# Hybrid decoder step: the last token group's FFN takes every other weight tile unsplit from its input and splits it on chip

## The chip, the cores and the metric

The kernel runs on one NeuronCore of one Trainium2 chip. The metric is the device time of one execution in microseconds (us); of several runs the median is taken. Besides the timed runs there is one profiled execution, and all durations, waits and clocks below come from its trace. In the trace PE is the matmul engine (PEld its weight loads), ACT the scalar engine, DVE the vector engine, and SP the engine from whose queue nearly all DMAs are issued. Tiles are named as in the program, with buffer numbers left out.

## The reference, cut to what matters

One layer of a decoder is applied to a prompt of 2048 tokens and to 8 single sample tokens. The first half of the layer mixes tokens (windowed attention beside a state-space scan); the second half is a SwiGLU FFN, and the change lies there:

```python
x = x + jnp.concatenate([a, s_out], axis=-1) @ w_out
h2 = rms_norm(x, norm2_w)
x = x + (jax.nn.silu(h2 @ w_gate) * (h2 @ w_up)) @ w_down   # 1024 -> 2816 -> 1024
...
yp = rms_norm(yp, final_norm_w)
```

All of it is float32.

## The kernel before

**Groups.** The tokens are cut into six groups that go one after the other through all stages: 256 tokens, four times 384, and last 264 (256 prompt tokens and the 8 samples). Each group needs all the weights again, since they don't fit on chip.

**Three matmuls for one.** The PE works in a faster, shortened float format. So each operand is split into a high part and a low rest, and a product is three matmuls: high by high, high by low, low by high (`mm3`). For an activation both parts come from ACT and DVE. For a weight tile there are two ways, both in `weight` (line 198):

- *raw*: a tile of 128x512 floats (256 KB; 128x384, 192 KB, for most of `wd`) is loaded from the input tensor into a buffer `wraw` (line 206, four buffers). ACT copies it, rounded, into the high half of a buffer `w` (line 207; the program's tag is `w2`, five buffers), and DVE subtracts that from the raw tile into the low half (line 209).
- *kept*: a tile that was split once has been stored to DRAM with both halves (line 213). From then on one DMA of 512 KB (384 KB for most of `wd`) fetches both halves into a `w` buffer (line 203), and ACT and DVE have nothing to do.

A third of the tiles is stored at its first use, a third at its second, a third at its third. So the first group takes all its tiles raw, the second and third take fewer and fewer, and from the fourth group on every tile is kept.

**The FFN stage** (`stage_f`, line 975). It goes through 22 blocks of 128 hidden features. For each, two tiles of the gate (`wg`) and then two of the up projection (`wu`) are multiplied into PSUM; ACT takes a tanh of the gate (line 1014), DVE multiplies (lines 1000, 1003), ACT and DVE split the result into the two halves of `hc` (lines 1004, 1008). The blocks form seven chunks, six of three and one of four. After the first block of a chunk, the down projection of the chunk before follows: eight `wd` tiles, each for one 128-row slice of the output, added to `x` by DVE (line 993). In the last group a `wg` or `wu` tile feeds 12 matmuls of 264 columns, a `wd` tile 9 (12 in the last chunk): 88 and 56 tiles, 144 in all, 1584 matmuls.

**Beside it.** While the last group's FFN begins, the final norm of the fifth group (`stage_z`) runs: two matmuls, a chain on ACT and DVE (lines 692 to 700), eight scalings on DVE (line 1041), and four stores of 384 KB from the SP queue (line 1043).

**Order.** A scheduler puts each engine's instructions into a fixed order when the program is built; each engine then works through its queue in that order. A load into a buffer waits until the buffer's last reader is done, and everything behind it in the SP queue waits too. With five `w` buffers, the load of a tile can be issued when the PE has finished the tile five places ahead of it.

Of the kernel before, what the change touches and what calls it, by code (L numbers as in the profile page):

```python
# [10 lines left out]
F32 = mybir.dt.float32  # L11
# [3 lines left out]
ALU = mybir.AluOpType  # L15
# [57 lines left out]
def hymba(ctx: ExitStack, tc: tile.TileContext, I: dict, O: dict, groups):  # L73
# [4 lines left out]
    NMAX = max(nb * P + (NS if s else 0) for nb, s in groups)  # L78
# [9 lines left out]
    def T(shape, dtype=F32, tag=None, bufs=1):  # L88
        cnt[0] += 1
        nm = f"{tag}_{cnt[0]}"  # L90
        return sb.tile(shape, dtype, tag=tag, name=nm, bufs=bufs)
# [5 lines left out]
    def DR(shape, tag, bufs=1):  # L97
        cnt[0] += 1
        return dr.tile(shape, F32, tag=tag, name=f"{tag}_{cnt[0]}", bufs=bufs)

    V, S, G, PE, SP = nc.vector, nc.scalar, nc.gpsimd, nc.tensor, nc.sync
# [83 lines left out]
    def later(n, fn):  # L185
        due.append((clock[0] + n, len(due) + cnt[0] * 1e-6, fn))
# [7 lines left out]

    wn, kept, seen = [0], {}, {}

    def weight(name, at, w=512):
        t = T([P, 1024], F32R, tag="w2", bufs=5)[:, :2 * w]  # L200
        hi, lo = t[:, :w], t[:, w:]
        if (name, at) in kept:
            SP.dma_start(t.bitcast(F32), kept[name, at])
            return hi, lo
        raw = T([P, 512], tag="wraw", bufs=4)[:, :w]
        SP.dma_start(raw, I[name][at] if name != "wd" else I[name][:, at:at + w])
        S.activation(hi, raw, AF.Copy)  # L207
        e = V
        e.tensor_tensor(lo, raw, hi.bitcast(F32), ALU.subtract)  # L209
        k = seen[name, at] = seen.get((name, at), len(seen) % 3) - 1  # L210
        if k < 0:
            d = kept[name, at] = DR([P, 2 * w], f"{name}{len(kept)}")
            later(2, lambda: SP.dma_start(d, t.bitcast(F32)))
        return hi, lo

    def std(name, u):

        r = []
        for h in range(2):
            hi, lo = weight(name, (u, h))  # L220
            r += [(hi[:, k * P:(k + 1) * P], lo[:, k * P:(k + 1) * P]) for k in range(4)]
        return r
# [751 lines left out]

    def stage_f(g):
        N, x1, h2 = g["N"], g["x1"], g["h2"]
        if not hid:
            hid.append(T([P, 2 * (FC + 1) * NMAX], F32R, tag="hc").rearrange("p (a o t) -> p a o t", a=2 * (FC + 1), o=1))
        hid3 = hid[0]

        def down(c, end=False):
            fs, n = chunks[c], len(chunks[c]) * P

            for ms in ([[0, 1, 2], [3], [4], [5], [6], [7]] if end else [[m] for m in range(KT)]):
                w = [weight("wd", c_off[c] + m * n, n) for m in ms]
                ps = [PS("d") for m in ms]
                jobs = [(i, m) for i in range(len(fs)) for m in range(len(ms))]
                for i, m in sorted(jobs, key=lambda e: (e[0] == len(fs) - 1, e[1], e[0])):
                    wi = tuple(t[:, i * P:(i + 1) * P] for t in w[m])
                    s = fs[i] % (FC + 1)  # L990
                    mm3(ps[m][:, :N], wi, (hid3[:, s], hid3[:, FC + 1 + s]), 0, N, i == 0, i == len(fs) - 1)
                for m, p in zip(ms, ps):
                    V.tensor_tensor(x1[:, m, :N], p[:, :N], x1[:, m, :N], ALU.add)  # L993
                    if end:
                        norm_sum(g, x1, sq, m, N, 0 if g is gs[-1] else 1)
                if ms[-1] % 4 == 3 or end:
                    yield
# [48 lines left out]
    gs, b0, off, prev = [], 0, 0, None  # L1046
    for nb, smp in groups:
        g = dict(nb=nb, smp=smp, b0=b0, off=off, N=nb * P + (NS if smp else 0), prev=prev)
        g["early"] = prev is None
        gs.append(g)  # L1050
        off += g["N"]
        b0 += nb
        prev = g
    assert b0 == NB
    n = len(gs)
    kinds = {"I": stage_x0, "X": stage_x, "A": stage_a, "K": stage_k, "B": stage_b, "P": stage_p, "Q": stage_q, "Y": stage_y,
             "S": stage_s, "O": stage_o, "H": stage_h, "F": stage_f, "Z": stage_z}
    made = {}

# [163 lines left out]
```

## Time and profile before

| | us |
|---|---|
| median of 3 runs (2373.48 to 2375.46) | 2374.78 |
| the profiled execution's own time | 2376.97 |
| its span in the trace | 2375.2 |
| PE busy, share of the span | 2290.4 (96%) |
| DVE busy | 1382.0 (58%) |
| ACT busy | 911.8 (38%) |
| bytes moved by DMA, mean rate | 628.96 MB, 265 GB/s |
| last group's FFN: first and last matmul start | 2151.2 and 2361.7 |

PE is marked busy for nearly all of the span, but its matmuls overlap in the record: one of 264 columns is shown for about 0.28 us, and the next starts 0.12 us after it when nothing is late. So the busy share hides short delays; the number of matmuls in a stretch against its length shows them. What ends the program after the last matmul of the FFN (norm, scaling, stores) takes about 13 us and is not touched.

### The profile page before, as it was taken

Reading aid. Unit: us, or ns where it says so; the run is one execution under the profiler, and the core shown is the slowest. Engines: PE = TensorE matmul, PEld = TensorE weight load, DVE = VectorE, ACT = ScalarE, POOL = GpSimd, SP = SyncE. Lnnn points to the kernel's source line nnn. Section 1 sums busy time; section 2 is a strip of 40 time slices with the busy share of each in tenths; the row PEclk is TensorE's granted clock in tenths of the full one; section 3 lists DMA queues with packets and bytes.
Section 4 is the critical chain, followed back from the end, with each engine's and each line's share of the span. In section 5 each row is a group of like instructions: output and inputs, shape, how many; then the busy total and the mean of one; then the engine's idle time right before and its main releaser. Section 6 shows DMA issues by size and latency. Waiting matters only on the chain.

```text
span 2375.2 us, 39240 instructions
## 1 busy us (share of the span) xinstructions
PE 2290.4 (96%) x14633; PEld 2230.5 (94%) x14633; DVE 1382.0 (58%) x3173; ACT 911.8 (38%) x1989; POOL 31.5 (1%) x109
## 2 busy tenths in 40 slices
PE   7999998999999999999999999999999999999997
PEld 6889887999999999999999999999989999998997
DVE  8987978665778555366745535554455574233223
ACT  6766666544436343332622332242233213122001
POOL 1000000000000000000000000000000000000000
PEclk9999999999999999999999999999999999999999
DMA  9766677888767778877887887777798798888997
GB/s 318 253 208 237 198 255 242 302 309 283 238 212 246 240 252 290 275 265 252 268 289 269 281 259 233 218 230 234 244 315 295 228 302 274 254 284 314 340 329 259
DMA packets 227226, 628.96 MB, mean 265 GB/s; under 512 B 24323, under 2 KB 57916, under 8 KB 226892
## 3 DMA queue, kind: packets, MB, share of 16 engines
q1 hardware_dynamic: 226892, 626.26, 79.4%
q8 instruction: 116, 1.90, 0.3%
q14 instruction: 74, 0.61, 0.1%
q10 hardware_dynamic: 144, 0.20, 0.0%
HBM read 516.67 MB, written 110.21 MB: 264 GB/s over the span
## 4 chain that ended last, share of the span: by engine, by line
PE 77%; DMA 11%; DVE 6%; ACT 3%; issue 2%; SPq 0%; ACTq 0%; DVEq 0%
PE psd L104 72%; PE psm L104 5%; DVE w L209 2%; DMA w<-wi 2%; DMA w<-wg 1%; DMA w<-wu 1%; DMA w<-wd 1%; DMA wraw<-in_wu_dram 1%; DMA wraw<-in_wg_dram 1%; ACT w L207 1%; DMA wraw<-in_wd_dram 1%; DMA wraw<-in_wi_dram 1%; ACT big L587 0%; DMA wraw<-in_wo_dram 0%; PE psm L607 0%
## 5 line engine op out<-in xcount | busy, mean ns | idle before, releaser
L104 PE MATMUL psd<-bhi,w 128*128 128x384 f32 (+1 forms) x4448 | 1089.0, 326 | 29.4 <-DVE w L209 8.5
L104 PEld LDWEIGHTS psd<-bhi,w 128*128 128x128 f32 x4448 | 781.9, 189 | 42.1 <-DVE w L209 12.4
L104 PE MATMUL psd<-blo,w 128*128 128x384 f32 (+1 forms) x2224 | 719.1, 324 | 0.1
L104 PE MATMUL psd<-hc,w 128*128 128x384 f32 (+2 forms) x3168 | 521.4, 321 | 15.6 <-DMA w<-wd 3.9
L104 PE MATMUL psd<-ahi,w 128*128 128x384 f32 (+1 forms) x2272 | 516.3, 314 | 20.6 <-DMA w<-wi 7.3
L104 PEld LDWEIGHTS psd<-hc,w 128*128 128x128 f32 x3168 | 496.8, 188 | 25.8 <-DVE w L209 5.2
L104 PEld LDWEIGHTS psd<-blo,w 128*128 128x128 f32 x2224 | 421.1, 189 | 1.4 <-DVE blo L338 0.3
L104 PEld LDWEIGHTS psd<-ahi,w 128*128 128x128 f32 x2272 | 386.2, 189 | 30.6 <-DMA w<-wi 7.1
L207 ACT ACTIVATE w<-wraw 128x512 fp32r<-128x512 f32 (+1 forms) x391 | 232.2, 602 | 338.4 <-PE psd L104 203.0
L104 PE MATMUL psd<-alo,w 128*128 128x384 f32 (+1 forms) x1136 | 355.5, 313 | 0.0
L209 DVE TENSOR_TENSOR w<-wraw,w 128x512 fp32r<-128x512 f32 (+1 forms) x391 | 252.9, 653 | 101.8 <-ACT w L207 98.3
L993 DVE TENSOR_TENSOR x<-psd,x 128x384 f32<-128x384 f32 (+2 forms) x336 | 168.5, 510 | 132.8 <-PE psd L104 132.1
L104 PEld LDWEIGHTS psd<-alo,w 128*128 128x128 f32 x1136 | 215.0, 189 | 1.5 <-issue 0.2
L1014 ACT ACTIVATE tmp<-psd 128x384 f32<-128x384 f32 (+2 forms) x132 | 59.8, 453 | 346.0 <-PE psd L104 345.9
L1000 DVE SCALAR_TENSOR_TENSOR tmp<-tmp,psd 128x384 f32<-128x384 f32 (+2 forms) x132 | 66.7, 505 | 176.3 <-ACT tmp L1014 176.2
L1003 DVE SCALAR_TENSOR_TENSOR tmp<-psd,tmp 128x384 f32<-128x384 f32 (+2 forms) x132 | 67.5, 512 | 167.2 <-PE psd L104 166.8
L1004 ACT ACTIVATE hc<-tmp 128x384 fp32r<-128x384 f32 (+2 forms) x132 | 64.4, 488 | 250.4 <-DVE tmp L1003 249.7
L381 DVE SCALAR_TENSOR_TENSOR x<-tmp,cols,x 128x384 f32<-128x384 f32 (+1 forms) x144 | 80.5, 567 | 37.9 <-ACT x L403 23.2
L317 ACT ACTIVATE tmp<-x 128x384 f32<-128x384 f32 (+2 forms) x84 | 40.5, 489 | 139.1 <-DVE x L941 102.1
L1008 DVE TENSOR_TENSOR hc<-tmp,hc 128x384 fp32r<-128x384 f32 (+2 forms) x132 | 67.6, 512 | 29.4 <-ACT hc L1004 29.3
L320 DVE TENSOR_TENSOR sq<-sq,tmp 128x384 f32<-128x384 f32 (+2 forms) x119 | 61.5, 517 | 34.9 <-ACT tmp L317 33.8
L587 ACT ACTIVATE big<-big,sm 128x256 f32<-128x256 f32 (+1 forms) x128 | 62.4, 489 | 20.8 <-DVE sm L581 20.6
(259 smaller groups left out, 1722.7 us busy)
## 6 DMA issues: line engine op xcount, KB each, us to landing
w<-wu SPq DMA_DIRECT2D x177, 512.0 KB, 4.6
w<-wg SPq DMA_DIRECT2D x175, 512.0 KB, 4.8
w<-wi SPq DMA_DIRECT2D x144, 512.0 KB, 4.9
w<-wd SPq DMA_DIRECT2D x192, 384.0 KB, 4.1
w<-wo SPq DMA_DIRECT2D x65, 512.0 KB, 4.5
wraw<-in_wg_dram SPq DMA_DIRECT2D x89, 256.0 KB, 3.6
wu<-w SPq DMA_DIRECT2D x44, 512.0 KB, 4.1
wg<-w SPq DMA_DIRECT2D x44, 512.0 KB, 3.4
```

Source lines behind the costliest of these rows:

```text
L104: PE.matmul(o, l, r, start=start, stop=stop)
L207: S.activation(hi, raw, AF.Copy)
L209: e.tensor_tensor(lo, raw, hi.bitcast(F32), ALU.subtract)
L320: e.tensor_tensor(sq[:, :N], sq[:, :N], t[:, :N], ALU.add)
L381: V.scalar_tensor_tensor(acc, raw[:, j:j + NP], cwc(j, t), acc, ALU.mult, ALU.add)
L587: S.activation(sc[kv][:, r, :W], sc[kv][:, r, :W], AF.Exp, bias=ng[:, h:h + 1], accum_out=den[:, h:h + 1])
L993: V.tensor_tensor(x1[:, m, :N], p[:, :N], x1[:, m, :N], ALU.add)
L1000: V.scalar_tensor_tensor(t[:, :N], t[:, :N], 1.0, pg[:, :N], ALU.add, ALU.mult)
L1003: V.scalar_tensor_tensor(t[:, :N], pu[:, :N], 0.5, t[:, :N], ALU.mult, ALU.mult)
L1004: S.activation(hh[:, 0, :N], t[:, :N], AF.Copy)
L1008: e.tensor_tensor(hl[:, 0, :N], t[:, :N], hh[:, 0, :N].bitcast(F32), ALU.subtract)
L1014: S.activation(t[:, :N], pg[:, :N], AF.Tanh, scale=0.5)
```

## The change

A flag `again` is set when the last group's FFN begins (its token count is below the maximum and its index above 2; no other group meets both). While it is set, every second call of `weight` takes the raw way although the kept copy exists: a DMA of 256 or 192 KB in place of 512 or 384 KB, then the copy on ACT and the subtraction on DVE. Nothing is stored again. Since each projection asks for an even number of tiles, these are the first of the two tiles of each `wg` and `wu` step, and the even ones of the eight `wd` tiles: 72 of 144. The values are the same. The rest of the diff only names things; all line numbers behind the function move by 3 or 4.

```diff
+    kept, seen, again, turn = {}, {}, [False], [0]
     def weight(name, at, w=512):
         t = T([P, 1024], F32R, tag="w2", bufs=5)[:, :2 * w]
         hi, lo = t[:, :w], t[:, w:]
-        if (name, at) in kept:
+        turn[0] += 1
+        if (name, at) in kept and not (again[0] and turn[0] % 2):
             SP.dma_start(t.bitcast(F32), kept[name, at])
             return hi, lo
...
         S.activation(hi, raw, AF.Copy)
-        e = V
-        e.tensor_tensor(lo, raw, hi.bitcast(F32), ALU.subtract)
+        V.tensor_tensor(lo, raw, hi.bitcast(F32), ALU.subtract)
+        if (name, at) in kept:
+            return hi, lo
...
     def stage_f(g):
         N, x1, h2 = g["N"], g["x1"], g["h2"]
+        again[0] = g["N"] < NMAX and g["i"] > 2
...
-        g["early"] = prev is None
+        g["early"], g["i"] = prev is None, len(gs)
```

**Place 1, the SP queue at the beginning of the last group's FFN**, where the fifth group's results are stored (`out_yT_dram`). Before:

```order
1334 L203 DMA w_3633_22668<-wu_2003_11659 128x1024
1335 L1043 DMA out_yT_dram<-x_3083_18836 128x2x384
1336 L203 DMA w_3634_22670<-wu_525_2923 128x1024
1337 L1043 DMA out_yT_dram<-x_3083_18836 128x2x384
1338 L203 DMA w_3636_22700<-wg_1308_7443 128x1024
1339 L1043 DMA out_yT_dram<-x_3083_18836 128x2x384
1340 L203 DMA w_3637_22702<-wg_2010_11703 128x1024
1341 L1043 DMA out_yT_dram<-x_3083_18836 128x2x384
```

The same place now (`wraw` is a raw tile, `w` a kept one):

```order
1337 L208 DMA wraw_22792<-in_wd_dram 128x384
1338 L205 DMA w_3640_22688<-wu_525_2923 128x1024
1339 L1047 DMA out_yT_dram<-x_3083_18836 128x2x384 x3
1340 L205 DMA w_3644_22723<-wg_2010_11703 128x1024
1341 L1047 DMA out_yT_dram<-x_3083_18836 128x2x384
1342 L208 DMA wraw_22821<-in_wd_dram 128x384
1343 L208 DMA wraw_22853<-in_wd_dram 128x384
1344 L205 DMA w_3649_22761<-wu_1319_7501 128x1024
```

Three stores now stand in a row ahead of the kept tile 3644 (the second `wg` tile of the fourth block), and the raw tiles stand about eight tiles ahead of their use: the raw `wd` tile 22792 is queued ahead of the kept `wu` tile 3640.

**Place 2, DVE around a down projection of the last group's FFN** (L1003 and L1008 are the last steps of a hidden block, L993 the addition of one of the eight `wd` results). Before:

```order
2698 L1003 SCALAR_TENSOR_TENSOR tmp_23498<-psd_23505,tmp_23498 128x264
2699 L1008 TENSOR_TENSOR hc_2636<-tmp_23498,hc_2636 128x264
2700 L1000 SCALAR_TENSOR_TENSOR tmp_23561<-tmp_23561,psd_23536 128x264
2701 L1003 SCALAR_TENSOR_TENSOR tmp_23561<-psd_23569,tmp_23561 128x264
2702 L1008 TENSOR_TENSOR hc_2636<-tmp_23561,hc_2636 128x264
2703 L1000 SCALAR_TENSOR_TENSOR tmp_23625<-tmp_23625,psd_23600 128x264
2704 L1003 SCALAR_TENSOR_TENSOR tmp_23625<-psd_23633,tmp_23625 128x264
2705 L1008 TENSOR_TENSOR hc_2636<-tmp_23625,hc_2636 128x264
2706 L993 TENSOR_TENSOR x_3504_21708<-psd_23662,x_3504_21708 128x264
2707 L993 TENSOR_TENSOR x_3504_21708<-psd_23675,x_3504_21708 128x264
2708 L993 TENSOR_TENSOR x_3504_21708<-psd_23688,x_3504_21708 128x264
```

Now, from the last hidden block's steps on:

```order
2743 L1004 SCALAR_TENSOR_TENSOR tmp_23736<-tmp_23736,psd_23711 128x264
2744 L210 TENSOR_TENSOR w_3797_23803<-wraw_23804,w_3797_23803 128x384
2745 L1007 SCALAR_TENSOR_TENSOR tmp_23736<-psd_23747,tmp_23736 128x264
2746 L210 TENSOR_TENSOR w_3802_23833<-wraw_23834,w_3802_23833 128x384
2747 L1012 TENSOR_TENSOR hc_2636<-tmp_23736,hc_2636 128x264
2748 L997 TENSOR_TENSOR x_3504_21708<-psd_23779,x_3504_21708 128x264
2749 L997 TENSOR_TENSOR x_3504_21708<-psd_23792,x_3504_21708 128x264
2750 L210 TENSOR_TENSOR w_3807_23862<-wraw_23863,w_3807_23862 128x384
2751 L997 TENSOR_TENSOR x_3504_21708<-psd_23808,x_3504_21708 128x264
2752 L997 TENSOR_TENSOR x_3504_21708<-psd_23821,x_3504_21708 128x264
```

The subtractions (L210) now stand between the hidden blocks' steps and between the additions: one for every raw tile, each at about the place where its `w` buffer comes free (the raw tile of the seventh result behind the addition of the second).

**Place 3, the SP queue at the end of the third group's FFN**, where the last raw tiles of before are loaded. Before:

```order
849 L206 DMA wraw_14405<-in_wd_dram 128x512
850 L203 DMA w_2417_14199<-wg_1758_10066 128x1024
851 L213 DMA wg_2420_14206<-w_2418_14201 128x1024
852 L203 DMA w_2424_14240<-wu_1027_5750 128x1024
853 L203 DMA w_2425_14242<-wu_1767_10111 128x1024
854 L213 DMA wd_2432_14288<-w_2430_14283 128x1024
```

Now:

```order
849 L208 DMA wraw_14405<-in_wd_dram 128x512
850 L205 DMA w_2417_14199<-wg_1758_10066 128x1024
851 L216 DMA wg_2420_14206<-w_2418_14201 128x1024
852 L208 DMA wraw_22496<-in_wg_dram 128x512
853 L205 DMA w_2424_14240<-wu_1027_5750 128x1024
854 L205 DMA w_2425_14242<-wu_1767_10111 128x1024
855 L216 DMA wd_2432_14288<-w_2430_14283 128x1024
856 L208 DMA wraw_22534<-in_wu_dram 128x512
```

The last group's first four raw tiles are loaded here, some 850 us ahead of their use, each behind the store of a tile whose split freed a `wraw` buffer; two of the four are shown.

## Rows read from the trace of the kernel before

**Rows 1.** Profile page: PE and DMA busy tenths in 40 slices of the span

```profile
PE   7999998999999999999999999999999999999997
...
DMA  9766677888767778877887887777798798888997
```

**Rows 2.** Busy time of each engine in three stretches of the last group's FFN

```profile
core 0: us, PE busy (x) PEld busy (x) DVE busy (x) ACT busy (x) POOL busy (x), PEclk, DMA share, GB/s
...
2151.00:2201.90 50.90, 46.75 (x366) 44.76 (x366) 17.13 (x39) 8.83 (x17) 0.00 (x0) 1.00 0.95 337
2201.90:2343.30 141.40, 135.31 (x1082) 131.56 (x1081) 36.24 (x85) 12.25 (x30) 0.00 (x0) 1.00 0.95 335
2343.30:2362.00 18.70, 17.71 (x144) 17.18 (x143) 7.64 (x18) 4.12 (x10) 0.00 (x0) 1.00 0.76 265
```

**Rows 3.** Timeline of PE in one down projection of it: start, us, count, [idle before]

```profile
2207.43 2.33 PE L104 MATMUL psd<-hc,w 128*128 128x264 f32 x18
...
2210.17 6.73 PE L104 MATMUL psd<-hc,w 128*128 128x264 f32 x54 [0.42 <-DMA w<-wd]
```

**Rows 4.** The chain of work that ended last, 2150 to 2362 us, by line

```profile
by line: PE psd L104 60.4%; DMA w<-wg 16.3%; DMA w<-wd 11.4%; DMA w<-wu 10.0%; issue 1.0%; SPq L203 0.4%; PE psm L104 0.3%; DVE tmp L1003 0.2%; DVE x L993 0.2%
```

**Rows 5.** DMA in the last group's FFN, 2151 to 2362: issues, KB each, us to landing

```profile
DMA packets 21413, 69.46 MB, mean 329 GB/s; under 512 B 2326, under 2 KB 3350, under 8 KB 21395
...
w<-wg SPq DMA_DIRECT2D x42, 512.0 KB, 5.6
w<-wu SPq DMA_DIRECT2D x42, 512.0 KB, 5.6
w<-wd SPq DMA_DIRECT2D x48, 384.0 KB, 4.5
```

**Rows 6.** The same view in the fifth group's FFN, 1870 to 2080

```profile
DMA packets 19490, 57.39 MB, mean 273 GB/s; under 512 B 2090, under 2 KB 3122, under 8 KB 19475
...
w<-wg SPq DMA_DIRECT2D x30, 512.0 KB, 4.4
w<-wu SPq DMA_DIRECT2D x30, 512.0 KB, 4.6
w<-wd SPq DMA_DIRECT2D x34, 384.0 KB, 4.7
```

**Rows 7.** SP queue in the last group's FFN: first and last of four stores

```profile
2162.39 0.39 SPq L1043 DMA_DIRECT2D out_yT_dram<-x  x1
...
2166.62 1.43 SPq L1043 DMA_DIRECT2D out_yT_dram<-x  x1
```

**Rows 8.** DVE timeline of the fifth group's final scaling

```profile
2161.21 4.32 DVE L1041 SCALAR_TENSOR_TENSOR x<-x,cols,sq 128x384 f32<-128x384 f32 x8
```

**Rows 9.** All splits of raw tiles in the run: ns min/median/max, first and last start

```profile
L207 ACT ACTIVATE w<-wraw x391: 506/630/641, 8.8 to 1293.9; 128x512 fp32r<-128x512 f32 x148, 128x384 fp32r<-128x384 f32 x48
L209 DVE TENSOR_TENSOR w<-wraw,w x391: 535/683/696, 11.0 to 1294.9; 128x512 fp32r<-128x512 f32 x148, 128x384 fp32r<-128x384 f32 x48
```

**Rows 10.** Profile page, DMA issues: raw tiles, KB each, us to landing

```profile
wraw<-in_wg_dram SPq DMA_DIRECT2D x89, 256.0 KB, 3.6
```

**Rows 11.** Two stretches of the first group's FFN, columns as in rows 2

```profile
366.00:394.00 28.00, 23.42 (x169) 20.62 (x168) 24.18 (x62) 14.90 (x38) 0.00 (x0) 1.00 0.73 243
405.00:432.00 27.00, 26.73 (x220) 26.16 (x219) 20.92 (x44) 14.70 (x28) 0.00 (x0) 1.00 0.88 286
```

**Rows 12.** Timeline of PE, a down projection of the first group with raw tiles only

```profile
424.58 8.44 PE L104 MATMUL psd<-hc,w 128*128 128x256 f32 x70
```

**Rows 13.** Timelines of ACT and DVE at the end of the first group's FFN

```profile
451.07 1.98 ACT L207 ACTIVATE w<-wraw 128x512 fp32r<-128x512 f32 x3 [1.57 <-DMA wraw<-in_wd_dram]
...
451.74 1.39 DVE L209 TENSOR_TENSOR w<-wraw,w 128x512 fp32r<-128x512 f32 x2 [1.45 <-ACT w L207]
453.04 0.42 DVE L1003 SCALAR_TENSOR_TENSOR tmp<-psd,tmp 128x256 f32<-128x256 f32 x1
```

**Rows 14.** The end of the third group's FFN, columns as in rows 2

```profile
1270.00:1304.00 34.00, 34.00 (x195) 33.66 (x194) 19.15 (x37) 12.44 (x25) 0.00 (x0) 1.00 0.69 240
```

More of the change, by code (lines that the diff above doesn't have):

```diff
@@ L193, in tick @@
             d[2]()
-    wn, kept, seen = [0], {}, {}
+    kept, seen, again, turn = {}, {}, [False], [0]
     def weight(name, at, w=512):
```

## Prediction

> **What bounds the kernel now.** The page's slices come first [rows 1]: PE is at nine tenths everywhere, and that hides more than it shows, since matmuls overlap in the record. So the next view is the one that counts matmuls in the stretches of the last group's FFN, the only stage that the change touches [rows 2]. Beside it stands the pace of an undisturbed run of matmuls there [rows 3]: 18 in a row of which the last one starts 2.33 - 0.28 = 2.05 us behind the first, 17 steps, so 0.1206 us each (the next 54 give (6.73 - 0.28) / 53 = 0.1217, with small delays in them). At 0.1206 the three stretches need
>
> - 366 x 0.1206 = 44.1 us, and took 50.9: 6.8 us lost;
> - 1082 x 0.1206 = 130.5 us, and took 141.4: 10.9 us lost, five chunks of about 2.2 each;
> - 144 x 0.1206 = 17.4 us, and took 18.7: 1.3 us lost.
>
> That is 19.0 us in which PE could have worked and did not, out of 211. The clock is not the reason: it was granted in full, 1.00, in all three. DMA is: its engines are busy for 0.95 of the first two stretches at 335 to 337 GB/s [rows 2], the wait inside the down projection is for a `wd` load [rows 3], and the chain of work that ended last runs for 37.7% of this stage through loads of `wg`, `wd` and `wu` [rows 4]. A kept tile is issued when the PE has finished the tile five places ahead of it, so four tiles of matmuls cover it: 4 x 12 x 0.1206 = 5.8 us for `wg` and `wu`, 4 x 9 x 0.1206 = 4.3 us for `wd`. They take 5.6 and 4.5 us to land [rows 5], as medians; about half come too late. **The last group's FFN is bound by its weight loads**, because its 264 columns give a tile of the same size less work than the 384 of the groups ahead of it. ACT and DVE are busy for 9% and 26% of the long stretch [rows 2].
>
> **The change part by part.** *Bytes.* 72 of 144 tiles shrink to half. A chunk of three blocks (12 `wg` and `wu` tiles, 8 `wd`) moves 12 x 512 + 8 x 384 = 9216 KB before; now 6 x 512 + 6 x 256 + 4 x 384 + 4 x 192 = 6912 KB, which is 7.08 MB in (144 + 72) x 0.1206 = 26.0 us if the PE isn't held: 272 GB/s. That is, nearly to the number, the rate of the fifth group's FFN, 273 GB/s [rows 6], so its landings serve as prices: 4.4 and 4.6 us for a kept `wg` or `wu` tile, inside the 5.8 us of cover; 4.7 us for a `wd` tile, 0.4 above the 4.3 of cover. There, however, eight `wd` loads of full size follow one another, and here every other one is half. The four kept `wd` tiles of a chunk cost between nothing and 4 x 0.4 = 1.6 us; I take 0.5, nearer to nothing since the burst is thinned. Over five chunks 2.5 us stay of 10.9 (0 to 8).
>
> *Raw tiles.* Their loads need a `wraw` buffer only, which frees when the tile four raw tiles earlier, eight tiles earlier in all, is split. So they stand far ahead of their use (place 1), and 3.6 us to land [rows 10] is covered several times. What counts is the split. It can start when the `w` buffer is free, and 0.63 us on ACT and 0.68 on DVE [rows 9], with a few tenths between them, make some 1.7 us against 4.3 or 5.8 of cover. In the order (place 2) each subtraction stands about where its buffer frees. Ahead of it at most a gating step or an addition waits for the PE, and what that one waits for is a tile at least four ahead of the one being split. In sum 72 x 0.63 = 45 us of ACT and 72 x 0.68 = 49 us of DVE at the most lie beside 200 us of matmuls, on engines that are mostly idle there. I cost them at nothing. The cover is gone if a split begins more than about 2.6 us late (4.3 - 1.7); then PE waits for DVE. The nearest row that speaks for nothing is the first group's: a down projection on raw tiles alone ran 70 matmuls of 256 columns at (8.44 - 0.28) / 69 = 0.118 us, without a stop [rows 12].
>
> *Behind the split.* In DVE's queue the last steps of a hidden block now wait behind a subtraction, and the down projection needs them. Inside the stage a whole block of 48 matmuls lies between. At the end, the last block's steps have 27 matmuls of the last down projection as cover, 27 x 0.1206 = 3.3 us; the one subtraction and copy add up to 1.3. Nothing.
>
> *The beginning.* Of the 6.8 us lost in the first stretch a part belongs to the fifth group's stores. SP waited for DVE's scaling, so that the first store went at 2162.39 and the last at 2166.62, with weight loads queued between (place 1) [rows 7], while the eight scalings ran for 4.32 us from 2161.21 [rows 8]. Now three stores stand in a row ahead of the kept tile 3644 (place 1), so this tile goes behind the sixth scaling: 2161.2 + 6 x 0.54 = 2164.5, and with two subtractions of 0.68 and a gating step, no longer than a scaling, between, up to 2166.4. It lands 4.5 us later, at 2169.0 to 2170.9. It is the 14th tile; a PE that isn't held reaches it at 2151.2 + 13 x 1.45 = 2170.0. So it is up to 0.9 us late, the next kept tile behind the fourth store and two raw tiles about as much again, and the stores' 1.6 MB still pass in these 10 us. I take 3.0 us as left of 6.8 (0 to 6.8).
>
> *The end and the early loads.* Of the last 1.3 us I leave 0.5 (0 to 1.3). The four raw loads in the third group's FFN (place 3) stand behind stores that waited for the very splits that free their buffers, so they block nothing; 1 MB there meets DMA engines at 0.69 busy while PE did 195 matmuls without idling [rows 14]. Nothing.
>
> *The sum.* 3.0 + 2.5 + 0.5 = 6.0 us of lost time stay of 19.0: **13.0 us are gained.** The profiled execution of 2376.97 would be 2364.0. The median of the runs lies 2.2 below that execution, 2374.78, so 2361.8. With all bounds at nothing left, the gain is 19.0 (2355.8); with all at their upper ends, 16.1 us stay and 2.9 are gained (2371.9).
>
> What the raw tile's DMA is worth in time, not in bytes, is where the Trainium skill speaks against this change. In this run a raw tile's load of 256 KB takes 3.6 us to land [rows 10], a kept one of 512 KB 4.4 us at a like rate [rows 6]: 18% less, not half. The skill's page "DMA: Bandwidth & Descriptors" (Anatomy of one DMA) gives each DMA a fixed part of about 2.0 us beside its bytes, and its section Bandwidth advises batches of 1 MiB or more; by its formula, an estimate, 3.2 us become 2.6, 19% less, which the rows bear out for a single landing. If transfers followed one another, the page would have a pair of tiles shrink by a tenth and not by a quarter, and the rival below would hold.
>
> **The rivals.** *Loads stay the bound in part.* If a halved tile occupies the engines for 18% less and not for half, a pair costs 0.91 of before; the DMA share of 0.95 at a chunk of 28.2 us (26.0 + 2.2) becomes 0.95 x 28.2 x 0.91 = 24.4 us of 26.0 available, 0.94, as crowded as before. Then the PE is again held by late kept tiles, perhaps half as much as now: 9.5 us gained, 2365.3. Against it: the fifth group's FFN moved as many bytes per us at landings of 4.4 to 4.7 [rows 6], and several loads are in flight at once.
>
> *Nothing to be seen.* The kept tiles' cover of four tiles stays short for `wd`, and the stores hold the SP queue at least as long as before: all upper ends together, 2.9 us gained, 2371.9. For it: the three stores in a row. Against it: `wg` and `wu` landings are the larger share of the chain [rows 4].
>
> *Slower: the split takes the place of the load.* DVE and ACT work in order. In the first group a subtraction waited 1.45 us for a copy that waited 1.57 for a raw load, and L1003, whose matmuls had long ended, began behind two of them at 453.04 [rows 13]. In a stretch of that group with DVE busy for 24.2 of 28 us, 169 matmuls took 28 us [rows 11], 0.166 each in place of 0.118. The mechanism decides from 19.0 / 72 = 0.26 us of PE wait for each raw tile; at 0.5 us the stage loses 36 and gains 19, so 2374.8 + 17 = 2392. Against it: these stretches had the next group's mixers on DVE and ACT and only raw tiles with their stores. When the mixers thinned out, 220 matmuls took 27 us [rows 11], 26.0 of them at 0.118: 1.0 lost. Here DVE is at 26% before and some 50% after.
>
> That the change does nothing of what it says can be left out: the order has 72 raw loads more, all for this stage.
>
> **How the numbers follow.** Forecast 2361.8, chance 0.68. Loads stay the bound in part, 2365.3: 0.15. Nothing to be seen, 2371.9: 0.11. Slower, 2392: 0.06. The range goes from 2355.5 (nothing left of the loss) to 2369.5, short of the last two cases. A measurement of this kernel can tell about 0.2%, 4.7 us, from no change. Faster by more than that is the forecast and the first rival, with a little over: 0.84. Within 0.2%: 0.11. Slower: 0.05, the rest of its case being small losses.
>
> **What would show it.** Right: in the last group's FFN the DMA share falls from 0.95 to about 0.75 to 0.85, the 1082 matmuls of its long stretch take some 133 us in place of 141, PE's waits for `wg` and `wu` loads nearly vanish, kept `wg` tiles land in about 4.5 us; what is late lies between 2165 and 2175 us, behind the stores. PE's waits for DVE L210 stay near zero. Wrong: kept tiles still land in over 5 us with a DMA share above 0.9 (first rival); PE waits for L210 in every chunk, or for `hc` at the down projections (third); the first stretch loses as much as before (second).

## The result, and the profile after

The changed kernel takes 2364.97 us (median of 6 runs, 2358.92 to 2366.72) against 2375.14 for the kernel before, run beside it. The ratio is 0.9943 with a 95% interval of 0.993 to 0.9955, so 10.7 to 16.6 us of 2375 are gained, 13.5 in the middle. The two medians alone lie 10.2 us apart (0.9957), just outside that interval; in the repeat beside other kernels, t1_change, they lie 13.6 apart. The forecast, 2361.8 of 2374.78, was a ratio of 0.9945.

The profiled execution took 2358.92 us (2364.0 was forecast; that of t1_change, the same kernel, took 2364.57), with a span of 2357.1, 18.1 less than before. Not all of that is the change. From the start of the first to the start of the last matmul of the last group's FFN (called *the stage* from here on) before takes from 2151.18 to 2361.74, 210.6 us; after takes from 2146.86 to 2343.94, 197.1. That is 13.5. Another 4.3 us lie ahead of the stage, where the change moves nothing but four early loads. In t1_change's trace the stage begins at 2152, later than in before, and takes 197.6 us. So the stage repeats within half a microsecond, the 2150 us ahead of it scatter by several, and the verdicts below go by the stage.

The page's slices of after, as [rows 1]:

```profile
PE   7999998999999999999999999999999999999997
...
DMA  9766677898767778777888887777788788887885
```

PE reads the same as before, digit for digit, although PE does the same matmuls in 13.5 us less. DMA's last four digits fall from 8, 9, 9, 7 to 7, 8, 8, 5. The view of [rows 2] for after (start:end, length, busy time and count of each engine, granted clock, DMA share, GB/s), in three stretches cut where before's were cut by time, though not at the same matmuls (the first holds 404 here, 366 in before):

```profile
core 0: us, PE busy (x) PEld busy (x) DVE busy (x) ACT busy (x) POOL busy (x), PEclk, DMA share, GB/s
2146.80:2197.40 50.60, 49.56 (x404) 48.67 (x403) 28.83 (x58) 19.37 (x37) 0.00 (x0) 1.00 0.86 281
2197.40:2325.90 128.50, 127.41 (x1051) 126.36 (x1050) 63.69 (x132) 37.52 (x78) 0.00 (x0) 1.00 0.83 270
2325.90:2344.10 18.20, 16.59 (x138) 16.32 (x136) 9.11 (x21) 5.35 (x13) 0.00 (x0) 1.00 0.44 143
```

At the pace of 0.1206 us the matmuls need 48.7, 126.8 and 16.6 us: 1.9, 1.7 and 1.6 us are lost, where before lost 6.8, 10.9 and 1.3. Cut at before's matmuls, by their starts in the trace, the long stretch takes 132.3 us in place of 141.5 and loses 2.1. DVE's busy share in the long stretch is 0.50 (63.69 of 128.5) and ACT's 0.29.

The DMA view of the stage, as [rows 5] (issues, KB each, median us to landing):

```profile
DMA packets 20800, 51.51 MB, mean 261 GB/s; under 512 B 2256, under 2 KB 6352, under 8 KB 20780
...
w<-wg SPq DMA_DIRECT2D x21, 512.0 KB, 4.4
...
w<-wd SPq DMA_DIRECT2D x24, 384.0 KB, 3.4
...
wraw<-in_wu_dram SPq DMA_DIRECT2D x19, 256.0 KB, 3.8
```

Kept `wg` tiles land in 4.4 us in place of 5.6, `wd` tiles in 3.4 in place of 4.5. The whole run moves 611.67 MB in place of 628.96: 17.3 MB less, which is 48 tiles shortened by 256 KB and 24 by 192.

The chain of work that ended last, from 2120 us on, as [rows 4] (start, duration, what), some pieces of it:

```profile
2162.28 0.61 DVE w L210
...
2168.27 5.12 DMA w<-wd
2173.44 30.53 PE psd L104 x252
2203.98 5.14 DMA w<-wg
2209.17 21.05 PE psd L104 x173
...
2335.44 4.08 DMA w<-wd
```

Up to 2162 the chain runs through the fifth group's norm, scalings and a few splits on ACT and DVE. From there on, where before's chain went through loads for 37.7% of the stage [rows 4], it meets one `wg` load per chunk (at 2203.98, and so on every 26 us, five in all), two `wd` loads, and one split on DVE at 2162.28. A piece's length is how long the load took, not how long PE stood still for it; that is in the view of waits (engine, line <- what it waited for: us in total, times, longest):

```profile
PEld psd L104 <- DMA w<-wg: 2.1, 5, 0.6
PE psd L104 <- DMA w<-wd: 2.1, 2, 1.6
...
PE psd L104 <- DMA w<-wg: 1.0, 4, 0.3
...
PEld psd L104 <- DVE w L210: 0.6, 1, 0.6
```

One late `wg` tile a chunk costs at most 0.6 us; the largest single hold, 1.6 us, is a `wd` load; of 72 splits one was late, by 0.6.

In t1_change's trace, the same kernel, the same split is late by 0.5 us, and in the five chunks behind it other loads are: a `wu` or `wg` tile three times (0.2 to 0.5 us), and a kept `wd` tile three times (0.5 to 0.6). The view of waits puts these three down to L210 too, because in each a subtraction for a later tile ends within 0.1 us of PE's start. But the `wd` tile that PE needs there landed 0.13 us ahead of PE each time (2238.44, 2262.91 and 2317.98), and in the second the weight load begins before that subtraction (2262.35, 0.69 us long) has ended:

```profile
2263.02 0.30 PEld L104 LDWEIGHTS psd<-hc,w 128*128 128x128 f32 x2 [0.54 <-issue]
```

So these are late loads.

### The profile page after: what moved, and what is told of

It is laid out like the page before. It is cut to its first block, busy times and chain, and to the rows that moved or that the text cites. A ratio compares the mean times of both kernels' runs of the same rounds, so it can differ in the third digit from the quotient of the medians.

```text
span 2357.1 us, 39548 instructions
## 1 busy us (share of the span) xinstructions
PE 2285.7 (97%) x14633; PEld 2229.6 (95%) x14633; DVE 1425.4 (60%) x3245; ACT 951.0 (40%) x2061; POOL 31.0 (1%) x109
## 2 busy tenths in 40 slices
DMA packets 227227, 611.67 MB, mean 259 GB/s; under 512 B 24323, under 2 KB 60988, under 8 KB 226892
## 4 chain that ended last, share of the span: by engine, by line
PE 73%; DMA 5%; DVE 1%; ACT 1%; issue 0%; SPq 0%; ACTq 0%; DVEq 0%
PE psd L104 69%; PE psm L104 4%; DMA w<-wi 2%; DMA w<-wg 1%; DMA w<-wd 1%; DVE x L1045 1%; PE psm L610 0%; DMA m<-in_sssm_dram 0%; DMA out_yT_dram<-x 0%; DMA m<-sbcd 0%; PE psm L730 0%; ACT L698 0%; ACT sq L695 0%; PE psm L737 0%; DVE sq L703 0%
## 5 line engine op out<-in xcount | busy, mean ns | idle before, releaser
L209 ACT ACTIVATE w<-wraw 128x512 fp32r<-128x512 f32 (+1 forms) x463 | 275.6, 601 | 418.6 <-PE psd L104 255.8
L210 DVE TENSOR_TENSOR w<-wraw,w 128x512 fp32r<-128x512 f32 (+1 forms) x463 | 300.2, 654 | 114.4 <-ACT w L209 108.4
L1008 ACT ACTIVATE hc<-tmp 128x384 fp32r<-128x384 f32 (+2 forms) x132 | 64.2, 486 | 181.3 <-DVE tmp L1007 180.8
```

The costliest lines, as they stand in the source:

```text
L210: V.tensor_tensor(lo, raw, hi.bitcast(F32), ALU.subtract)
L1008: S.activation(hh[:, 0, :N], t[:, :N], AF.Copy)
```

## The experiments

"Lost" is the stage's length less 191.6 us: 1583 steps from matmul to matmul at the prediction's pace of 0.1206 us, 190.9, and 0.65 for the two matmuls of the fifth group's norm between them. Bytes, rate and DMA share are those of the stage.

In the kernels that use the attention's buffers (tag `big`) the last tile, with twelve matmuls, lies in one of them. The expectations that name the stage of such a kernel (192.8 us for e3, 191.4 for e7) stop at the last matmul that reads a `w` buffer and are 1.4 to 1.5 us too short; the table counts to the last matmul. In e3_more_buffers it is in this row, which begins at 2342.06:

```profile
2342.06 1.62 PE L104 MATMUL psd<-hc,big 128*128 128x264 f32 x12
```

| kernel | what it is | stage, us | lost | MB | GB/s | DMA share |
|---|---|---|---|---|---|---|
| before | all kept, 5 buffers | 210.6 | 19.0 | 69.44 | 330 | 0.93 |
| after | every other tile raw | 197.1 | 5.5 | 51.51 | 261 | 0.80 |
| t1_change | after again | 197.6 | 6.1 | | | |
| e1_all_raw | all raw | 192.9 | 1.4 | 34.62 | 179 | 0.61 |
| e2_half_load | bytes of after, no split | 201.0 | 9.4 | 52.34 | 260 | 0.83 |
| e5_six_buffers | all kept, one tile in six in idle buffers | 198.6 | 7.0 | 67.57 | 340 | 0.95 |
| e3_more_buffers | all kept, 9 buffers | 194.3 | 2.7 | 67.31 | 346 | 0.93 |
| e4_split_twice | after, splits doubled | 201.5 | 9.9 | 51.61 | 256 | 0.80 |
| e6_late_norm | after, norm and stores later | 196.0 | 4.4 | 51.50 | 263 | 0.80 |
| e7_both, t3_both | after with 9 buffers | 192.9 | 1.3 | 49.81 | 258 | 0.79 |
| t4_groups_4_to_6 | raw from the fourth group on | 195.1 | 3.5 | 51.50 | 264 | 0.81 |
| b1_all | t4, and 9 buffers at the end | 192.9 | 1.3 | 49.82 | 258 | 0.78 |

The bytes, rates and shares of e7_both are those of t3_both, the same kernel. Where a kernel is named without a ratio, it was run once.

**Is the split a cost, or was it bytes?** If splits press on ACT and DVE, taking all tiles raw must cost; if loads are the bound, it must gain more.

```diff
-        if (name, at) in kept and not (again[0] and turn[0] % 2):
+        if (name, at) in kept and not again[0]:
```

> The last group's FFN takes all 144 weight tiles raw, not every other one; nothing else is altered. Measure: the stage from its first to its last matmul, 210.7 us before, 197.1 with the change, 191 if PE were never held. Bytes theory (the stage was late because its loads moved too many bytes): bytes fall once more by a third, the DMA share to about 0.55, waits for w loads are gone, 193 to 196 us. Split theory (what is left with the change is the price of splitting on ACT and DVE): twice as many splits, 199 us or more, with PE waiting for the subtraction.

The stage takes 192.9 us, just below the range of the bytes theory. Its only holds, 2.0 us in all, lie 17 to 20 us behind its beginning, where the fifth group's scalings stand between the splits on DVE; the second of them ends behind a split on ACT whose raw `wu` load came late. The waits of e1_all_raw from 2160 to 2176 us:

```profile
PEld psd L104 <- DVE w L210: 1.3, 1, 1.3
PE psd L104 <- DVE w L210: 1.1, 1, 1.1
PEld psd L104 <- ACT w L209: 0.8, 1, 0.8
```

From there its chain is one run of 1428 matmuls in 171.66 us, 0.1202 each. So twice the splits cost nothing in steady state, and the rival that the split takes the place of the load falls.

**Is it the bytes alone?** The tiles that the change takes raw are loaded at half size, from the kept copy, straight into a `w` buffer: the bytes of the change, no split, and the issue as late as before. The kernel leaves out the product of the low half; its matmuls read the high half again.

```diff
+        if (name, at) in kept:
+            SP.dma_start(hi.bitcast(F32), kept[name, at][:, :w])
+            return hi, hi
```

> The 72 tiles that the change takes raw are loaded as the high half of the kept copy alone (256 or 192 KB), straight into the w buffer, with no split; the matmuls of their low half read the high half again, so the low part's product is left out. As many bytes as the change, no work on ACT and DVE, and each load waits for its w buffer, four tiles ahead, as before. Bytes theory: 195 to 199 us for the stage. Lookahead theory (the change gains because a raw load stands eight tiles ahead of its use, not because it is small): 203 us or more.

The stage takes 201.0 us, between the two expected ranges. The window of the stage, and one group of its loads in the DMA view:

```profile
2156.17:2357.17 201.00, 195.04 (x1586) 191.86 (x1584) 60.70 (x140) 25.12 (x57) 0.00 (x0) 1.00 0.83 260
```

```profile
w<-wg SPq DMA_DIRECT2D x21, 512.0 KB, 6.8
```

With the change's bytes and rate but without its early issue, 9.6 of the 13.5 us are gained. The full `wg` tiles even take 6.8 us to land. So bytes are not the whole of it. What is left between the two kernels is that a raw tile is requested eight tiles ahead and doesn't wait for its `w` buffer; that is the likely source of the rest, some 4 us. Why the full `wg` tiles landed so late here, at no higher a rate, is open.

**Is it bytes at all?** All tiles stay kept and full, but every other one goes into one of four buffers that the attention uses earlier and that lie idle in this stage. Of the nine buffers the five cover a load with nine tiles and the four with seven, at the bytes of before.

```diff
-        t = T([P, 1024], F32R, tag="w2", bufs=5)[:, :2 * w]
+        t = (T([P, 1024], F32R, tag="big", bufs=4) if again[0] and turn[0] % 2 else T([P, 1024], F32R, tag="w2", bufs=5))[:, :2 * w]
...
-        if (name, at) in kept and not (again[0] and turn[0] % 2):
+        if (name, at) in kept:
```

> All tiles kept as before, but in the last group's FFN every other tile lies in four buffers of the attention (tag big, idle by then), so nine buffers in place of five: loads can be issued some eight tiles ahead. Bytes as before, no split. Bytes theory: 69 MB at 335 to 345 GB/s take 201 to 207 us, so 203 to 209 for the stage, DMA share 0.95 or more. Lookahead theory: 198 or less.

The window of its stage; then its DMA view, with the rate in 40 slices of the stage and two landings:

```profile
2149.10:2343.39 194.29, 193.17 (x1586) 192.49 (x1586) 60.73 (x140) 25.22 (x57) 0.00 (x0) 1.00 0.93 346
```

```profile
GB/s 277 340 289 396 393 407 409 407 404 359 327 353 396 403 356 302 326 386 414 390 315 351 294 415 395 382 300 340 395 413 383 305 316 374 417 406 405 270 48 2
DMA packets 20821, 67.31 MB, mean 346 GB/s; under 512 B 2259, under 2 KB 3283, under 8 KB 20803
...
w<-wg SPq DMA_DIRECT2D x20, 512.0 KB, 5.9
...
w<-wd SPq DMA_DIRECT2D x24, 384.0 KB, 5.4
```

This is the run that overturns a reading of the prediction. The DMA engines are as busy as before, 0.93; the loads land no sooner, 5.9 and 5.4 us; and 2.7 us are lost in place of 19.0. No load holds PE any more: its one hold, 1.5 us, is at the very end behind the last block's `hc`. The rate of before was not the most that the engines give: 346 GB/s in the mean, over 400 in many slices. Before was held because the time from issue to landing was about as long as the work of four tiles, and a load can't be issued earlier than its buffer is free.

How little is missing shows a kernel in which one tile in six goes into the idle buffers, so that the other five have five tiles of cover (5 x 1.45 = 7.2 us for `wg` and `wu`). The sixth rotates through four buffers and is mostly requested much earlier: a `wg` tile issued at 2197.84 is used at 2228.43.

```diff
+        t = (T([P, 1024], F32R, tag="big", bufs=4) if again[0] and turn[0] % 6 == 5 else T([P, 1024], F32R, tag="w2", bufs=5))[:, :2 * w]
...
+        if (name, at) in kept:
```

> All tiles kept as before; in the last group's FFN one tile in six lies in a buffer of the attention (tag big), the other five in the five w buffers, so a load can be issued one tile earlier: five tiles of matmuls cover it, 7.2 us for wg and wu, 5.4 for wd, in place of 5.8 and 4.3; bytes as before. With nine buffers the stage took 192.8 us, before it took 210.7. Lookahead theory (a load was late by the little that its landing of 5.6 and 4.5 us exceeds its cover): most of the gain is there already, 194 to 199 us. Bytes theory: 204 or more.

```profile
2153.07:2351.65 198.58, 195.17 (x1586) 192.53 (x1586) 60.61 (x140) 25.12 (x57) 0.00 (x0) 1.00 0.95 340
```

Its stage is 12.0 us shorter than before's, with nearly before's bytes and no split. One tile more of cover for five loads in six, and more for the sixth, is worth nearly what 72 splits and 17 MB less are worth (13.5).

**How much room has the split?** The copy and the subtraction are made twice.

```diff
         if (name, at) in kept:
+            S.activation(hi, raw, AF.Copy)
+            V.tensor_tensor(lo, raw, hi.bitcast(F32), ALU.subtract)
+        if (name, at) in kept:
             return hi, lo
```

> The change, with the copy on ACT and the subtraction on DVE of each of the 72 raw tiles done twice in a row: 45 us more on ACT, 49 more on DVE, 1.3 us more ahead of each raw tile. If the splits are covered (my prediction: some 2.6 us to spare for each): 197 to 199 us for the stage. If splitting costs PE something already: 202 or more.

The stage takes 201.5 us, between the two expected ranges. It grows by 4.4 us over after's, but in one place. Windows of e4_split_twice:

```profile
2165.00:2169.00 4.00, 3.92 (x32) 3.71 (x32) 4.00 (x9) 1.55 (x4) 0.00 (x0) 1.00 0.44 115
2169.00:2172.50 3.50, 0.57 (x5) 0.36 (x3) 3.50 (x8) 1.86 (x4) 0.00 (x0) 1.00 1.08 339
2172.50:2180.00 7.50, 6.70 (x31) 6.27 (x31) 3.62 (x8) 1.93 (x5) 0.00 (x0) 0.55 0.88 307
2180.00:2190.00 10.00, 10.00 (x84) 10.00 (x84) 7.11 (x16) 4.89 (x11) 0.00 (x0) 0.99 0.64 195
```

and its timeline of PE there (start, us, count, [idle before <- releaser]):

```profile
2172.23 0.39 PE L104 MATMUL psd<-ahi,w 128*128 128x264 f32 x1 [2.93 <-ACT w L212]
```

DVE is busy without a gap from 2165 to 2172.5, with the eight scalings among the doubled splits, and PE stands for 3 us. Then the granted clock falls to 0.55 for 7.5 us. Behind 2180 the doubled splits cost nothing that shows. So 1.3 us more ahead of each raw tile are covered in steady state, within the 2.6 us to spare that the prediction gave a split; beside the fifth group's norm they aren't.

**Is the loss at the beginning the norm's?** The fifth group's norm and stores are begun 24 units of the FFN later.

```diff
+            run(("F", i), units=24)
             run(("F", i), ([("Z", i - 1)], 1))
```

> The change, but the fifth group's final norm, scaling and stores begin 24 steps later, in the middle of the last group's FFN. With the change 2.3 us of that stage are lost between 2162 and 2173, where the split of a raw tile stood behind the scalings on DVE and three stores in a row held the SP queue. If the stores in a row cost this: the loss moves with them, the beginning runs without a stop, and the stage takes 196 to 198 us as with the change. If it is the beginning itself (loads not yet ahead): some 2 us stay between 2160 and 2175.

The stage takes 196.0 us, and its chain is one run of matmuls up to 2174. The norm's scalings and stores now stand between 2223 and 2232, and there two holds follow them, 1.0 us behind an addition on DVE and 0.5 behind the `wg` load below; a third, 0.9 us behind the `wu` load, lies ahead of them:

```profile
2119.88 54.55 PE psd L104 x381
...
2179.42 6.09 DMA w<-wu
...
2231.54 6.70 DMA w<-wg
...
2335.74 3.63 DMA w<-wd
```

So most of the loss at the beginning belongs to the norm and the stores wherever they stand, and moving them gains only 1 to 1.5 us.

**Both ways together.** After's raw tiles, with the kept ones in the idle buffers, so that both have seven tiles of cover or more:

```diff
-        t = T([P, 1024], F32R, tag="w2", bufs=5)[:, :2 * w]
+        t = (T([P, 1024], F32R, tag="big", bufs=4) if again[0] and turn[0] % 2 else T([P, 1024], F32R, tag="w2", bufs=5))[:, :2 * w]
```

> The change, and the kept tiles of the last group's FFN in the attention's four buffers, so that the raw tiles have the five w buffers for themselves: half the bytes for 72 tiles and about eight tiles of lookahead for all. Lookahead theory: with nine buffers alone the stage took 192.8 us; fewer bytes add nothing, 192 to 194.5, and the 0.3 to 0.6 us that a wg tile is late in each chunk are gone. If bytes matter beside it: 191 to 192.

No load and no split is late any more: 192.9 us. A piece of the chain of t3_both, the same kernel, as long as nearly the whole stage:

```profile
2157.41 187.87 PE psd L104 x1547
```

These are 0.1214 us per matmul, with small delays in them that no engine is waited for. e1_all_raw, with five buffers, comes to the same 192.9 us in spite of its holds, because its matmuls follow each other at 0.1202; why the pace differs is open. Against e3_more_buffers, 194.3, the 1.4 us less are about the hold behind `hc`, which isn't there; they are no sign that bytes matter beside the cover.

**The candidates, timed side by side.** t1_change is after, t2_more_buffers is e3_more_buffers, t3_both is e7_both, and t4 sets the flag from the fourth group on:

```diff
-        again[0] = g["N"] < NMAX and g["i"] > 2
+        again[0] = g["i"] > 2
```

> The change itself, timed beside the next three: 13 us below the kernel before (ratio 0.9945), the stage 197 us.

> Nine buffers and all tiles kept, without any split: the stage took 192.8 us in the look at it, 17.9 below before. Lookahead theory: ratio 0.9925, 4 us faster than the change.

> The change with nine buffers: the stage took 191.4 us, 19.3 below before. Ratio 0.992, 5 to 6 us faster than the change, 1 to 1.5 us faster than nine buffers alone (which is about what the runs can tell apart).

> The change in the FFN of the fourth and fifth group too, whose tiles feed matmuls of 384 columns: four tiles cover a load for 4 x 12 x 0.173 = 8.3 us there, and loads land in 4.4 to 4.7. Lookahead theory: nothing to gain in these two stages, so as the change within 3 us, or slower where the splits meet the next group's mixers on DVE (up to 10 us). Bytes theory: as these stages run at a DMA share of 0.84, a further gain of 5 us or more.

Before took 2376.19 us (median) beside them.

| kernel | median, us | ratio to before, 95% |
|---|---|---|
| t1_change | 2362.61 | 0.9941 (0.9929 to 0.9954) |
| t2_more_buffers | 2359.47 | 0.9924 (0.9911 to 0.9938) |
| t3_both | 2359.05 | 0.9927 (0.9913 to 0.9941) |
| t4_groups_4_to_6 | 2351.9 | 0.9896 (0.9882 to 0.991) |

The profiled execution of t2 took 6949 us with slow matmuls from end to end, so e3's trace stands for it. By time t1, t2 and t3 are too near one another for their intervals; by the stage, t3 is 4.8 us ahead of t1, and t2, by e3's trace, 3.3.

t4 was not expected to gain so much. In the fourth group's own FFN it gains nothing: 265.3 us against 265.1 before, from the first to the last matmul of its down projections. A matmul of 384 columns takes 0.173 us (18 in a row in 3.28, the last of them shown for 0.34), four tiles are 4 x 12 x 0.173 = 8.3 us of cover, and at that width loads land in 4.4 to 4.7 us [rows 6]. But the flag, once set, isn't taken back before the next FFN, so the projections between the fourth and the fifth group's FFN, among them the last group's, take every other tile raw too. The stretch there, from the last matmul of the fourth group's FFN to the first down projection of the fifth's, before and then t4:

```profile
1722.50:1865.40 142.90, 137.37 (x932) 133.12 (x932) 74.97 (x211) 44.04 (x99) 6.90 (x20) 0.99 0.86 289
```

```profile
1722.80:1857.80 135.00, 134.41 (x933) 131.19 (x932) 93.89 (x245) 62.34 (x133) 10.28 (x20) 1.00 0.70 240
```

and PE's waits for the input projection's tiles in it, before and t4:

```profile
PE psd L104 <- DMA w<-wi: 4.5, 4, 3.0
```

```profile
PE psd L104 <- DMA w<-wi: 0.6, 2, 0.3
```

7.9 us are gained there, and PE's waits for `wi` loads fall by 3.9 of them. That points to the same shortage as in the stage, a late load with little cover, and to the same cure; no run takes the rest apart. The fifth group's FFN gains little: 281.7 us from the first to the last matmul of its down projections against 283.0 in t1_change.

**The version that beats both.** t4's flag, and the idle buffers in the last group's FFN:

```diff
+        t = (T([P, 1024], F32R, tag="big", bufs=4) if again[0] == 2 and turn[0] % 2 else T([P, 1024], F32R, tag="w2", bufs=5))[:, :2 * w]
...
+        again[0] = 0 if g["i"] < 3 else 2 if g is gs[-1] else 1
```

> The run on groups 4 to 6 gained 10 us beyond the change, but not in the FFN stages: 8 us of it lie in the input and output projections between the fourth and fifth group's FFN, most of them for the last group, at 264 columns, which took the raw way too since the flag stays set between FFN stages. Here that, and in the last group's FFN the attention's four buffers beside the five. Lookahead theory: the two add up, 2351.9 less the 4 to 5 us that nine buffers were worth beside the change: 2346 to 2349, ratio 0.988. If they don't add up (the same DMA time gained twice): 2350 to 2352.

Median 2350.91 us of 6 runs (2347.86 to 2357.53) against 2375.91 for before: ratio 0.9889 (0.9871 to 0.9908), about 26 us gained. Its stage takes 192.9 us and the projections 135.5. It has the lowest ratio of all kernels run, but by time it can't be told from t4 (0.9896), and the median lies in the range expected if the two gains don't add up. Its stage is 2.2 us shorter than t4's; the 4 to 5 us expected were counted from after's stage, which is longer than t4's.

## Why the prediction was right, and where it wasn't

**The bound.** That weight loads hold the last group's FFN was right: 19.0 us were lost, as the prediction counted, and with nine buffers and nothing else altered (e3_more_buffers) 16.3 of them are gone and no load holds PE. Not all 19.0 could be had: the shortest stages take 192.9 us, 17.7 below before. The comparison of cover with landing (5.8 and 4.3 against 5.6 and 4.5) named the cause. What it put first, the DMA share of 0.95 at 335 GB/s [rows 2] as a sign of a limit, was no evidence: over the whole stage e3_more_buffers has before's share, 0.93, moves 346 GB/s in place of 330, and loses 2.7 us. The trace gave this sum with four tiles of cover, and the prediction didn't ask what a fifth would do.

The Trainium skill says as much in "Perfetto Trace Analysis" (Identifying the Most-Contended Engine): the busy share of the 16 DMA engines misleads, and one should compare the rate with the memory's peak instead. The first half agrees with these traces (0.93 in before and in e3). The second would not have told the two apart: the Trainium skill's page "DMA: Bandwidth & Descriptors" (Specifications) gives about 358 GB/s per core, half of what the two cores of a stack share, by which before's 330 are 0.92 and e3's 346 are 0.97, an estimate; for this kernel on one core it is no ceiling, since e3's slices at over 400 lie above it. The Trainium skill's page "Perfetto Trace Analysis" (Optimization Strategy) also says that a gap that repeats through a stretch can mean too few buffers; e5_six_buffers and e3_more_buffers bear that out with 12.0 and 16.3 us. The prediction's formula for a single DMA is the fit that the Trainium skill's page "DMA: Bandwidth & Descriptors" (Anatomy of one DMA) gives for DMAs issued from GpSimd; the loads here are issued from SP, and nothing in the sum goes by it.

**Bytes and landings.** The forecast of 272 GB/s and 4.4 us was met by 270 GB/s in the long stretch and 4.4 us for `wg`. The DMA share was to be 0.75 to 0.85; it is 0.83 in the long stretch and 0.80 over the stage. The sign held. e2_half_load puts what fewer bytes alone give at 9.6 of 13.5 us, though not for every tile by shorter landings: its full `wg` tiles took 6.8. The likely source of the rest, that raw tiles are requested eight tiles ahead, stood in the prediction as a reason why they cost nothing, not as a gain of its own.

**The split.** Costed at nothing, measured at 0.6 us in one place (0.5 in t1_change). DVE's timeline in after at the beginning:

```profile
2157.62 2.73 DVE L1045 SCALAR_TENSOR_TENSOR x<-x,cols,sq 128x384 f32<-128x384 f32 x5
...
2160.61 1.67 DVE L1045 SCALAR_TENSOR_TENSOR x<-x,cols,sq 128x384 f32<-128x384 f32 x3
2162.20 0.68 DVE L210 TENSOR_TENSOR w<-wraw,w 128x512 fp32r<-128x512 f32 x1
```

The subtraction stands behind all eight scalings, and PE waits for it at 2162.3. The prediction followed SP's queue past the scalings and the stores; DVE's own queue behind the same scalings it passed over. e1_all_raw and e4_split_twice show how this grows, to single waits of 1.3 and 3 us.

**The beginning.** 3.0 predicted as left, 1.9 measured. SP's queue in after:

```profile
2158.80 2.83 SPq L1047 DMA_DIRECT2D out_yT_dram<-x  x3
2161.72 0.68 SPq L205 DMA_DIRECT2D w<-wg  x1
2162.48 0.91 SPq L1047 DMA_DIRECT2D out_yT_dram<-x  x1
2163.49 1.50 SPq L208 DMA_DIRECT2D wraw<-in_wd_dram  x2
2165.08 0.79 SPq L205 DMA_DIRECT2D w<-wu  x1
...
2168.27 0.33 SPq L205 DMA_DIRECT2D w<-wd  x1
```

The kept `wg` tile behind the three stores went at 2161.72, 14.9 us into the stage; 13.3 to 15.2 was predicted. It was not late after all. Late were those behind the fourth store, the `wu` tile of 2165.08 and the `wd` tile of 2168.27, by 0.5 and 0.7 us. The mechanism was right (e6_late_norm moves it with the norm), its size was under the value taken.

**The steady part.** 2.5 predicted, 1.7 measured; cut at the same matmuls as before's long stretch, 2.1, and 2.7 in t1_change. The 132.3 us of these matmuls meet the 133 that were forecast. The prediction feared `wd` tiles, whose cover seemed 0.4 us short. In after's trace they land in 3.4 us, and one `wg` tile a chunk is late instead, by up to 0.6; in t1_change's, three of the six late tiles are `wd` tiles. Which tile is late differs between two executions of one kernel; the size is about that of the forecast.

**The end.** This term was mis-sized: 0.5 predicted, 1.6 measured, no less than the 1.3 of before. PE's timeline of after, behind the last full run:

```profile
2339.65 4.56 PE L104 MATMUL psd<-hc,w 128*128 128x264 f32 x36 [1.61 <-DMA w<-wd]
```

The last down projection takes its first three `wd` tiles together, all the matmuls of the older blocks ahead of those of the last one. So these buffers are freed only as the group of three ends, and the load issued then, at 2335.44, has at most two tiles of cover (2 x 12 x 0.1206 = 2.9 us) against 4.08 to landing. The prediction had seen that order, as cover for `hc`, and had not asked what it does to the buffers. e2_half_load (3.47 us on the chain at 2348.93) and e6_late_norm show the same load late; with nine buffers it no longer is.

**The sum.** That 13.0 predicted and 13.5 measured lie so near each other is in part luck: the beginning was put 1.1 us too high and the steady part up to 0.8, the end 1.1 too low, and the split's 0.6, put at nothing, lies within the beginning.

**The rivals.** Loads bound in part: its number, 2365.3, is nearer to the median of 2364.97 than the forecast is, so the median alone doesn't exclude it. The ratio that it meant, 0.9960, lies outside the intervals of the change (0.993 to 0.9955) and of t1_change (0.9929 to 0.9954), and it had the stage gain 9.5 us where 13.5 were measured, 13.0 in t1_change. A chunk was to fill the DMA engines to 0.94 as before; they are at 0.83, and the 261 GB/s went through with kept tiles landing in 4.4 us. By share and length of the stage the engines were busy for about 0.8 of the time of before (0.80 x 197.1 against 0.93 x 210.6), nearer to the 0.75 of a pair's bytes than to the rival's 0.91. Nothing to be seen, and slower: both excluded by the interval (0.9988 and 1.007 would have been their ratios); PE waits for L210 once in each of the two traces.

**Not settled.** The early raw loads in the third group's FFN had no run of their own; the 4.3 us by which after's stage begins sooner are scatter by t1_change, and a small effect of these loads would be hidden in it. Which tiles of the projections give t4's gain was not taken apart.

## What to carry to other kernels

When loads hold a stage, set the time from issue to landing against the work that a load's buffers let it be issued ahead of; the DMA share doesn't tell the two cases apart. Idle buffers that give most loads one tile more of cover did nearly what shortening every other load did (198.6 us and 197.1), and nine buffers did more with less work (194.3). Look for the same shortage wherever an instruction works on few columns: here an FFN with 384 columns had nothing to give, while the stretch of projections ahead of the fifth group's FFN gave 7.9 us.

## What the runs showed of the hardware

The DMA engines of this core moved over 400 GB/s (up to 417 in a slice of 4.9 us, e3_more_buffers) and 346 in the mean over 194 us, at a busy share of 0.93; before had 330 at the same share. The same share of busy time was not the same rate.

In e4_split_twice PE did 5 matmuls in 3.5 us, after a long time at full clock. The granted clock was 0.55 over the 7.5 us that followed, mostly the lower of its two levels (1.2 GHz in place of 2.4): by its timeline 31 matmuls there, one each 0.22 us where 0.12 is the pace, and 0.99 again in the next 10 us. So a hold of 3 us cost about 3 us more behind it; the holds of up to 1.6 us in after left the clock at 1.00.
